# The last 128 gated tokens of each half stay on chip, two units move ahead of half B's last down block, and a norm gets four row tiles

## The chip, the cores and the metric

One core of a Trainium2 chip. The time is that of one execution on the device in microseconds (us), as the median of several runs; one execution is recorded by the hardware profiler. PE is TensorE (matmul), DVE is VectorE, ACT is ScalarE, POOL is GpSimd, SP is SyncE, which here only issues DMAs.

## The reference

A trunk of two layers over 1024 tokens of 1024 numbers, each with a feed-forward network (FFN) behind it, and a last norm. Layer 0 mixes tokens with a gated MLP and with running means, layer 1 is an RWKV-7 time mixing. All is fp32. What the change touches is the end of the time mixing:

```python
y = wkv7_scan(rh, decay, kh, vh, -kk, kk * ah)
mean = jnp.mean(y, axis=-1, keepdims=True)
var = jnp.mean(jnp.square(y - mean), axis=-1, keepdims=True)
y = ((y - mean) * lax.rsqrt(var + GN_EPS)).reshape(bsz, seq, d)
y = y * ln_w.astype(f32) + ln_b.astype(f32)
bonus = jnp.sum(rh * kh * r_k.astype(f32), axis=-1, keepdims=True) * vh
y = (y + bonus.reshape(bsz, seq, d)).astype(h.dtype)
return (y * g) @ w_o, v_first
...
def swiglu(hn, w_gate, w_up, w_down):
    return (jax.nn.silu(hn @ w_gate) * (hn @ w_up)) @ w_down
```

The scan runs over the tokens one after the other, 16 heads of 64. The residual `x + ...` follows, then `rms_norm` and `swiglu` with 2816 hidden columns.

## The kernel before

**Halves.** The 1024 tokens are worked on as half A (0 to 511) and half B (512 to 1023). Arrays lie with the features on the 128 partitions and the tokens along the row, as 8 tiles of 128 x 512 for a half.

**Products.** Every fp32 operand is split into a high and a low part (`split`, L159 to L162: ACT copies the high part, DVE subtracts it for the low one), and a product is three matmuls, high by high, high by low and low by high (`mm3`, L440 to L444, and `quarter`, L777 to L779). A matmul is 128 x 128 by 128 x 512.

**Weights.** Weights of 512 KB come from DRAM into one of three tiles `raw` by DMAs that ACT issues (`load_at`, L125), and are split into `whi` and `wlo`, three tiles each. Their order is a plan that is written out by hand ahead of the work (`push`, `push_units`, `push_o`, `push_act`), and `take` asks for the next one. `o` is the output projection's weight: eight pieces (`m` = 0 to 7), each of four DMAs of 128 KB.

**Order.** Each engine works through its own queue in order. A scheduler sets that order from a modelled time of each instruction, within priorities (`high_priority`) and waits that the code gives; PE's dense work is in the order of the code in some places.

**The recurrence.** `recur(h, ...)` runs the time mixing of a half as 8 chunks of 64 tokens. It is a generator that `drive` steps on beside dense FFN work, so many pieces of the one per piece of the other (`ratio`). After every second chunk `post(jj)` norms the result of 128 tokens (`ysb`), with the reciprocal root by POOL (`rsqrt`, L447), and `turn_out` transposes it on PE (L1540), multiplies by the gate on DVE into `gch` (L1784) and stores 128 tokens in DRAM (`y_d[h]`, L1787). The `yp` products of a chunk are copied to `ysb` by ACT (L1690), which is where this chain starts.

**The output projection.** It needs all 512 tokens of `y`. Four pieces of `y_d[h]` (two of the eight feature tiles each, 512 tokens) come back through `raw`, are planned by `push_act`, and are split by `take_act` into `ahi` and `alo`. `out_proj` then does 8 x 8 products with `o`, and each result is added to the residual `h` (L540).

**Half A.** The recurrence of half A runs beside the layer-0 FFN of half B; the last down block of that FFN (`steps_b`) runs out as the recurrence ends. Then come `project_norm` (the norm of half B for its time mixing, whose row sums are the matmuls of L477 and whose broadcast is L494), the output projection of A, low-rank products and gates of half B (`project_gate`), and `norm_a`: the norm of half A for its FFN by `norm_split` (L510), whose eight rows are scaled by DVE into one of two tiles (tag `nsq`), split, and spilled to `n_d[1]`. The first FFN units of half A use them at once. Mixing rows (L1231, L1238) of half B's projections run on DVE and ACT beside it.

**Half B.** The recurrence of half B runs beside the layer-1 FFN of half A. Near the end, `AHEAD_IN` = 2 units of a second step (`first_steps`, tiles `mm<-ahi,whi` of L777) stand ahead of the last down block of A (48 matmuls), four units behind it, three pieces of y between them. Then come the output projection of half B and the remaining six units beside the norm of half B.

Of the kernel before, what the change touches and what calls it, by code (L numbers as in the profile page):

```python
# [16 lines left out]
P = 128  # L17
# [25 lines left out]
LATER = (5, 6, 7, 8, 9, 10)  # L43
AHEAD_IN = 2


@with_exitstack
def tile_trunk(
# [56 lines left out]
    def col(c):  # L105
        return vec[:, c : c + 1]
# [8 lines left out]
    def push(key, parts, view=lambda t: t, dest=None):  # L115
        plan.append((key, parts, view, dest))

    def load_at(i):
        if i >= len(plan) or i in raws:
            return  # L120
        if plan[i][0][0] in acts and plan[i][0][0] not in dests:
            return
        raw = wst.tile([P, D], F32, tag="raw", name="raw")
        for dst, src in plan[i][1]:
            act.dma_start(dst(raw), src)  # L125
        raws[i] = raw
# [148 lines left out]

    def push_act(key, src):

        acts.add(key)
        for i in range(4):
            yield push((key, i), [(lambda raw: raw.rearrange("p (k t) -> p k t", k=2), src[:, 2 * i : 2 * i + 2, :])],  # L280
                 dest=lambda i=i: dests[key](i))

# [74 lines left out]
    o_first[0]()  # L357
    list(push_act(("y", 0), y_d[0]))
    push_beside(1, [lambda: None] + o_first[1:] + push_f(1, 0, G1A[0]))
# [9 lines left out]
    def push_units(units, between=iter(())):  # L369
        for i, n in units:  # L370
            push(("first1", i, n), push_pair(1, i, n, 0))
            next(between, None)
            next(between, None)

    for e in ffn_events(TAIL, True):
        if e == ("d", TAIL[-1]):
            push_units(UNITS[:AHEAD_IN])
        if e[0] != "d":
            push_ffn_event(1, 0, *e)
    y1 = push_act(("y", 1), y_d[1])  # L380
    push_units(UNITS[AHEAD_IN : AHEAD_IN + 3])
    for unit in (UNITS[AHEAD_IN + 3], None, None):
        next(y1)
        if unit:
            push_units([unit])
    next(y1)
    for go in push_o(1):
        go()
    push_units(UNITS[AHEAD_IN + 4 :])
    for f in range(2 * LATER[0]):  # L390
# [111 lines left out]

    def norm_split(h, c0, pool_, spill=None, b=None):

        if b is None:
            b = norm_scale(h)
        hi, lo = act_tiles(pool_)
        for k in range(KT):
            hn = nt.tile([P, HT], F32, tag="nsq", bufs=2, name="hn")
            dve.scalar_tensor_tensor(  # L510
                out=hn, in0=H[h][:, k, :], scalar=col(c0 + k), in1=b, op0=ALU.mult, op1=ALU.mult
            )
# [1004 lines left out]

    def recur(h, wp, stream, ratio):

# [202 lines left out]
        def post(jj):  # L1722
# [48 lines left out]
            def turn_out():  # L1771
                for q in range(2):
                    o = pst("sm")
                    for i in range(4):
                        p = 4 * q + i // 2 * 2
                        ordered(
                            pe.transpose, o[:, i * P : (i + 1) * P],
                            ysb[i % 2][:, p : p + 2, :].rearrange("t p d -> t (p d)"), ident,
                        )
                    ov = o.rearrange("p (q c r t) -> p q r c t", q=2, c=2, r=2)  # L1780
                    for i in range(4):
                        m = q * 4 + i
                        g = gch[:, m, :].rearrange("p (c t) -> p c t", c=2)
                        dve.scalar_tensor_tensor(  # L1784
                            out=g, in0=ov[:, i // 2, 1 - i % 2], scalar=col(C_LNB + m), in1=g, op0=ALU.add, op1=ALU.mult,
                        )
                sp.dma_start(y_d[h][:, :, jj * P : (jj + 1) * P], gch)  # L1787

# [20 lines left out]
        for c in range(8):  # L1809
            if c % 2 == 1:  # L1810
                pieces[:] = [post(c // 2)]
                next(pieces[0])
            open_[0] = (99, 1)[c % 2]
            bkt, w1 = yield from burst(c, bkt, w1)
            yield BURST
        for _ in pieces[0]:
            yield 0.3
        turned.pop()()
        yield 1.0

# [232 lines left out]
    prime_b()  # L2053
    drive(ffn(0, 1, nxt["hn"], f, D0P[:3], nd=2), recur(0, wp, in_pieces(hb_pool, 1, h_d[1, 0]), 6.2), 6.2)
    wp_es.close()
# [33 lines left out]
    def norm_a(gate):  # L2089
        got = []  # L2090
        between = [lambda: None] * KT
        between[0] = lambda: got.append(row_sums(sums))

        def rows_():
            with tc.high_priority(offset=AHEAD):
                got.append(norm_rows(got[0]))

        between[4] = rows_
        with tc.manual_schedule(engines={mybir.EngineType.PE}):
            gate(between)  # L2100
        with tc.high_priority(offset=AHEAD):
            hnA.extend(norm_split(0, C_FFN + 8, (yhi, y), n_d[1], got[1]))

# [13 lines left out]
    f, f_es = open_pool(name="ffn2", bufs=1, side="right")  # L2117
    hnA = nxt["hn"]
    all_units = [(i, 2 * i, n, True) for i, n in UNITS]
    dense_a = ffn(  # L2120
        1, 0, hnA, f, TAIL, early=True, after=lambda m: sp.dma_start(hs_d[0][:, m, :], H[0][:, m, :]),
        then={TAIL[-1][-1]: lambda: first_steps(all_units[:AHEAD_IN], hnA, f, "first1", hid1_d, True)},
    )
    drive(dense_a, recur(1, wp, in_pieces(hp, 0, h_d[0, 1]), RATIO), RATIO)
    for e in (wp_es, hp_es, f_es, ps_es):
        e.close()
    ps_es = open_psum("psd2", DENSE)
    f, f_es = open_pool(name="ffn3", bufs=1, side="right")
    xa, xa_es = open_pool(name="xa", bufs=1, side="left")
    xb, xb_es = open_pool(name="xb", bufs=1, side="left")  # L2130
    b, b_es = open_pool(name="act3", bufs=1, side="left")
# [4 lines left out]

    def y_calls():
        for call in range(8):
            if call > 4:
                next(got_y)  # L2140
            yield

    exhaust(first_steps(all_units[AHEAD_IN : AHEAD_IN + 4], hnA, f, "first1", hid1_d, between=y_calls()))
    exhaust(got_y)
    acc, add = running_sums(1)

# [175 lines left out]
```

## Time and profile before

| | us |
|---|---|
| median of three runs | 2373.31 |
| lowest and highest | 2365.13, 2375.23 |
| the profiled execution | 2372.49 |
| its span | 2370.8 |
| PE busy in it | 2283.6 |
| DVE busy | 1552.3 |
| ACT busy | 952.7 |
| POOL busy | 181.8 |

The span is the time from the first to the last recorded instruction. Places in the profile are in us from the start of the span. Three of them matter here: 1236 to 1310 (end of half A's recurrence, its output projection, up to the gate), 1323 to 1349 (norm of half A), 1772 to 1803 (end of half B's recurrence and what follows). An entry such as [8.82 <-ACT ahi L161] behind an instruction says that its engine was idle for 8.82 us before it, and that the instruction of ACT at L161 that writes `ahi` let it go on. ACTq and SPq are DMA issues of the two engines.

### The profile page before, as it was taken

The page shows a single profiled execution, that of the slowest core. Times are in us where ns is not written, and L with a number is a line of the kernel's source. Part 1 is how long each engine was busy: PE and PEld are TensorE (multiplying, and loading weights), DVE is VectorE, ACT ScalarE, POOL GpSimd, SP SyncE. Part 2 cuts the span into 40 slices and gives each one's busy share as a digit, 9 for nine tenths or more (in the row PEclk, how much of TensorE's full clock was granted, in tenths as well). Part 3 has the DMA queues.
Part 4 walks back from the last instruction along what each step waited for, and adds up shares of the span by engine and source line. Part 5 has one row for each costly group of instructions (what it writes and reads, how often), then busy time and mean ns, then how long its engine had stood idle before and what let it go on. Part 6 is the DMA issues. An engine that isn't in the chain of part 4 may idle for free. (4 is left out here: it accounts for less than half of the span.)

```text
span 2370.8 us, 37920 instructions
## 1 busy us (share of the span) xinstructions
PE 2283.6 (96%) x15171; PEld 1861.3 (79%) x15171; DVE 1552.3 (65%) x2496; ACT 952.7 (40%) x1507; POOL 181.8 (8%) x207
## 2 busy tenths in 40 slices
PE   8999999999999999999989899999999999999998
PEld 6888888888888877778767678777777887787886
DVE  6445775555567957767767857766664564776565
ACT  6233443443223764433335655533333442332014
POOL 0200000000000022201100122200110000000002
PEclk9999999999999999999999999999999999999999
DMA  5114473333765465776445375676546674547342
GB/s 183 54 45 141 152 196 98 107 107 121 286 234 200 149 187 146 210 219 195 129 141 154 121 211 152 194 232 175 161 147 212 203 249 142 169 151 257 125 160 98
DMA packets 427985, 392.04 MB, mean 165 GB/s; under 512 B 96992, under 2 KB 358240, under 8 KB 425120
## 3 DMA queue, kind: packets, MB, share of 16 engines
q1 hardware_dynamic: 174752, 202.68, 26.9%
q10 hardware_dynamic: 251840, 182.74, 25.9%
q0 software_dynamic: 1216, 4.20, 0.8%
q8 instruction: 119, 1.95, 0.3%
q14 instruction: 58, 0.48, 0.1%
HBM read 283.25 MB, written 106.30 MB: 164 GB/s over the span
## 5 line engine op out<-in xcount | busy, mean ns | idle before, releaser
L161 ACT ACTIVATE whi<-raw 128x1024 fp32r<-128x1024 f32 (+2 forms) x274 | 265.1, 974 | 394.2 <-PE mm L443 212.0
L162 DVE TENSOR_TENSOR wlo<-raw,whi 128x1024 fp32r<-128x1024 f32 (+2 forms) x274 | 314.1, 1151 | 164.8 <-ACT whi L161 135.8
L443 PE MATMUL mm<-alo,whi 128*128 128x512 f32 x864 | 342.2, 396 | 2.4 <-DVE alo L162 2.1
L442 PE MATMUL mm<-ahi,whi 128*128 128x512 f32 x832 | 329.4, 399 | 13.1 <-ACT ahi L161 11.5
L444 PE MATMUL mm<-ahi,wlo 128*128 128x512 f32 x832 | 328.7, 395 | 2.9 <-DVE wlo L162 2.9
L540 DVE TENSOR_TENSOR h<-h,mm 128x512 f32<-128x512 f32 x268 | 180.4, 685 | 133.8 <-PE mm L444 125.0
L777 PE MATMUL mm<-ahi,whi 128*128 128x512 f32 x488 | 193.0, 396 | 5.6 <-ACT whi L161 5.2
L442 PEld LDWEIGHTS mm<-ahi,whi 128*128 128x128 f32 x832 | 157.1, 189 | 50.7 <-ACT ahi L161 12.8
L443 PEld LDWEIGHTS mm<-alo,whi 128*128 128x128 f32 x864 | 163.3, 189 | 41.2 <-DVE alo L162 5.7
L778 PE MATMUL mm<-alo,whi 128*128 128x512 f32 x488 | 191.1, 392 | 0.0
L779 PE MATMUL mm<-ahi,wlo 128*128 128x512 f32 x488 | 188.7, 391 | 0.0
L444 PEld LDWEIGHTS mm<-ahi,wlo 128*128 128x128 f32 x832 | 157.2, 189 | 38.5 <-DVE wlo L162 3.8
L442 PE MATMUL mm<-hd,dhi 128*128 128x512 f32 x368 | 144.4, 392 | 1.1 <-DVE h L540 1.1
L444 PE MATMUL mm<-hd,dlo 128*128 128x512 f32 x368 | 143.4, 390 | 0.0
L443 PE MATMUL mm<-hd,dhi 128*128 128x512 f32 x368 | 143.2, 389 | 0.0
L777 PEld LDWEIGHTS mm<-ahi,whi 128*128 128x128 f32 x488 | 92.4, 189 | 26.8 <-ACT whi L161 6.1
L161 ACT ACTIVATE dhi<-raw 128x1024 fp32r<-128x1024 f32 x40 | 40.5, 1052 | 171.7 <-PE mm L443 135.6
L778 PEld LDWEIGHTS mm<-alo,whi 128*128 128x128 f32 x488 | 92.5, 190 | 19.4 <-issue 0.5
L779 PEld LDWEIGHTS mm<-ahi,wlo 128*128 128x128 f32 x488 | 92.3, 189 | 19.5
L442 PEld LDWEIGHTS mm<-hd,dhi 128*128 128x128 f32 x368 | 69.1, 188 | 16.3 <-DVE h L540 1.9
L444 PEld LDWEIGHTS mm<-hd,dlo 128*128 128x128 f32 x368 | 69.1, 188 | 14.5
L443 PEld LDWEIGHTS mm<-hd,dhi 128*128 128x128 f32 x368 | 69.1, 188 | 14.4 <-issue 0.2
(438 smaller groups left out, 4762.7 us busy)
## 6 DMA issues: line engine op xcount, KB each, us to landing
raw<-in_ffn_w_down_dram ACTq DMA_DIRECT2D x76, 512.0 KB
hid_d<-hid SPq DMA_DIRECT2D x69, 512.0 KB
raw<-in_ffn_w_gate_dram ACTq DMA_DIRECT2D x68, 512.0 KB
raw<-in_ffn_w_up_dram ACTq DMA_DIRECT2D x68, 512.0 KB
hd<-hid_d SPq DMA_DIRECT2D x56, 512.0 KB
ar<-ab_d SPq DMA_DIRECT2D x16, 1024.0 KB
raw<-in_ab_w_in_dram ACTq DMA_DIRECT2D x16, 512.0 KB
raw<-in_ab_w_out_dram ACTq DMA_DIRECT2D x16, 512.0 KB
```

Of the source, the lines that this page charges most:

```text
L161: act.activation(hi, src, AF.Copy)
L162: (eng or dve).tensor_tensor(out=lo, in0=src, in1=hi.bitcast(F32), op=ALU.subtract)
L442: pe.matmul(o, whi, xhi, start=first, stop=False)
L443: pe.matmul(o, whi, xlo, start=False, stop=False)
L444: newest[0] = pe.matmul(o, wlo, xhi, start=False, stop=last).ins
L540: dve.tensor_tensor(out=H[h][:, m, :], in0=H[h][:, m, :], in1=o, op=ALU.add)
L777: pe.matmul(o, wh[:, k, :], x[0][:, k, :], start=st, stop=False, skip_group_check=True)
L778: pe.matmul(o, wh[:, k, :], x[1][:, k, :], start=False, stop=False, skip_group_check=True)
L779: pe.matmul(o, wl[:, k, :], x[0][:, k, :], start=False, stop=k == 3, skip_group_check=True)
```

## The change

The first three parts of `y` that `turn_out` gives (tokens 0 to 383 of a half) go to DRAM as before. The fourth (`jj` = 3) is written to two on-chip tiles `yend` of 128 x 4 x 128, one for each four feature tiles, and `split_end` splits it into the last 128 columns of `ahi` and `alo`, at high priority. The pieces that come back from DRAM have 384 tokens. In half A, `yend` lies in a pool of its own; in half B, in the two tiles of tag `nsq`.

Of the four DMAs of each weight `o`, the second and fourth are issued by SP.

`AHEAD_IN` is 4, so four units stand ahead of half B's last down block and two behind it, with the pieces of y between these. In the recurrence of half B the last pause is put elsewhere: the transposes of `turn_out` are ordered behind the newest dense matmul after 2.7 pieces more of dense work.

`norm_a` uses the two `yend` tiles for rows 0, 1, 4 and 5, beside the two `nsq` tiles for the others. Two pools (`xa` and `xb`) are opened in the other order. Line numbers of the changed code are 5 or 6 lower in this part (L535 for L540, L1751 for L1756), and higher at the end.

```diff
-AHEAD_IN = 2
+AHEAD_IN = 4
...
-            act.dma_start(dst(raw), src)
+        for n, (dst, src) in enumerate(plan[i][1]):
+            (sp if plan[i][0][0] == "o" and n % 2 else act).dma_start(dst(raw), src)
...
-    def push_act(key, src):
+    def push_act(key, src, n=HT):
...
-            yield push((key, i), [(lambda raw: raw.rearrange("p (k t) -> p k t", k=2), src[:, 2 * i : 2 * i + 2, :])],
+            yield push((key, i), [(lambda raw: raw.rearrange("p (k t) -> p k t", k=2)[:, :, :n], src[:, 2 * i : 2 * i + 2, :n])],
...
-    list(push_act(("y", 0), y_d[0]))
+    list(push_act(("y", 0), y_d[0], HT - P))
...
-    y1 = push_act(("y", 1), y_d[1])
-    push_units(UNITS[AHEAD_IN : AHEAD_IN + 3])
-    for unit in (UNITS[AHEAD_IN + 3], None, None):
-        next(y1)
-        if unit:
-            push_units([unit])
-    next(y1)
+    push_units(UNITS[AHEAD_IN : AHEAD_IN + 2], push_act(("y", 1), y_d[1], HT - P))
...
-    push_units(UNITS[AHEAD_IN + 4 :])
+    push_units(UNITS[AHEAD_IN + 2 :])
...
-            hn = nt.tile([P, HT], F32, tag="nsq", bufs=2, name="hn")
+            pl, tag = extra if extra and k % 4 < 2 else (nt, "nsq")
+            hn = pl.tile([P, HT], F32, tag=tag, bufs=2, name="hn")
...
-                        g = gch[:, m, :].rearrange("p (c t) -> p c t", c=2)
+                        g, to = (t.rearrange("p (c t) -> p c t", c=2) for t in (gch[:, m, :], end(m) if jj == 3 else gch[:, m, :]))
...
-                sp.dma_start(y_d[h][:, :, jj * P : (jj + 1) * P], gch)
+                if jj != 3:
+                    sp.dma_start(y_d[h][:, :, jj * P : (jj + 1) * P], gch)
...
-            yield BURST
+            if c < 7 or not h:
+                yield BURST
...
+        if h:
+            yield 2.7 * ratio
+            last.append(newest[0])
         turned.pop()()
...
+    def split_end(ys, ends):
+        with tc.high_priority(offset=AHEAD):
+            for q, t in enumerate(ends):
+                split(t, *(y[:, 4 * q : 4 * q + 4, HT - P :] for y in ys))
...
         yield from take_act(("y", h))
+        split_end(ys, end_a.tiles)
...
-            hnA.extend(norm_split(0, C_FFN + 8, (yhi, y), n_d[1], got[1]))
+            hnA.extend(norm_split(0, C_FFN + 8, (yhi, y), n_d[1], got[1], (yhi, "yend")))
...
-    exhaust(first_steps(all_units[AHEAD_IN : AHEAD_IN + 4], hnA, f, "first1", hid1_d, between=y_calls()))
+    exhaust(first_steps(all_units[AHEAD_IN : AHEAD_IN + 2], hnA, f, "first1", hid1_d, between=got_y))
     exhaust(got_y)
+    split_end(ys, end_b.tiles)
```

How this moves instructions, by the order in which each engine has them (xN counts equal ones in a row). On ACT, at the end of half A's recurrence, where `nsq<-h` (L455, after it L449) belongs to `project_norm`, before:

```order
L455 ACTIVATE nsq<-h 128x512 x5
L125 DMA raw<-y_d_81 128x1024 x3
L455 ACTIVATE nsq<-h 128x512 x2
L161 ACTIVATE ahi<-raw 128x1024 x2
L125 DMA raw<-y_d_81 128x1024
L161 ACTIVATE ahi<-raw 128x1024
L125 DMA raw<-in_rwkv_w_o_dram 64x4x128 x4
L161 ACTIVATE ahi<-raw 128x1024
```

and after:

```order
L125 DMA raw<-y_d_81 128x2x384
L161 ACTIVATE ahi<-raw 128x2x384
L446 ACTIVATE nacc<-h 128x512
L449 ACTIVATE nsq<-h 128x512
L125 DMA raw<-y_d_81 128x2x384
L449 ACTIVATE nsq<-h 128x512 x2
L161 ACTIVATE ahi<-raw 128x2x384
L161 ACTIVATE ahi<-yend 128x4x128 x2
L449 ACTIVATE nsq<-h 128x512
L125 DMA raw<-y_d_81 128x2x384
L125 DMA raw<-in_rwkv_w_o_dram 64x4x128 x2
L161 ACTIVATE ahi<-raw 128x2x384
```

The first piece of y (not in these rows) and the next two are loaded and split ahead of the end of the norm's squares; only the fourth load stands behind the splits of `yend`.

On SP, from there on (`h<-h_d` reloads half A's residual, `h_d<-h` stores half B's), before:

```order
L2050 DMA h_d_86<-h 128x512 x5
L1787 DMA y_d_81<-gch 1024x1x128
L2050 DMA h_d_86<-h 128x512 x3
L2071 DMA h<-h_d_83 128x1024 x4
L515 DMA n_d_88<-hn 128x512 x8
```

and after:

```order
L2067 DMA h_d_86<-h 128x512 x7
L125 DMA raw<-in_rwkv_w_o_dram 64x4x128 x3
L2067 DMA h_d_86<-h 128x512
L125 DMA raw<-in_rwkv_w_o_dram 64x4x128 x9
L2089 DMA h<-h_d_83 128x1024 x4
L125 DMA raw<-in_rwkv_w_o_dram 64x4x128 x2
L510 DMA n_d_88<-hn 128x512 x8
```

The store of the last 128 tokens is gone, and the reload of the residual stands behind 14 transfers of `o` (two of them ahead of these rows).

On DVE, in the norm of half A, before:

```order
L510 SCALAR_TENSOR_TENSOR hn<-h,vec,aux 128x512
L162 TENSOR_TENSOR alo<-hn,ahi 128x512
L1238 SCALAR_TENSOR_TENSOR mix<-hn_11129,vec,mix 128x512 x2
L510 SCALAR_TENSOR_TENSOR hn<-h,vec,aux 128x512
L162 TENSOR_TENSOR alo<-hn,ahi 128x512
L1231 TENSOR_TENSOR xlo<-mix,xhi 128x512 x2
```

and after:

```order
L505 SCALAR_TENSOR_TENSOR hn<-h,vec,aux 128x512 x3
L1226 TENSOR_TENSOR alo<-mix,ahi 128x512
L505 SCALAR_TENSOR_TENSOR hn<-h,vec,aux 128x512
L1226 TENSOR_TENSOR alo<-mix,ahi 128x512
L162 TENSOR_TENSOR alo<-hn,ahi 128x512 x3
L1233 SCALAR_TENSOR_TENSOR mix<-hn_11134,vec,mix 128x512
L162 TENSOR_TENSOR alo<-hn,ahi 128x512
L505 SCALAR_TENSOR_TENSOR hn<-h,vec,aux 128x512
```

Rows come in groups, and part of the mixing stands behind them.

On DVE, at the end of half B's recurrence (`h<-h,mm` are the down block's additions to the residual), before:

```order
L540 TENSOR_TENSOR h<-h,mm 128x512 x3
L1756 SCALAR_TENSOR_TENSOR mean<-mean,var 128x16
L1762 TENSOR_TENSOR ysb<-ysb,var 128x512
L1763 TENSOR_TENSOR ysb<-ysb,mean 128x512
L1766 TENSOR_TENSOR ysb<-ysb,lnw 128x512
L1767 TENSOR_TENSOR ysb<-ysb,vch 128x512
L1766 TENSOR_TENSOR ysb<-ysb,lnw 128x512
L1767 TENSOR_TENSOR ysb<-ysb,vch 128x512
L1784 SCALAR_TENSOR_TENSOR gch<-sm,vec,gch 128x128 x8
```

and after:

```order
L535 TENSOR_TENSOR h<-h,mm 128x512 x3
L1751 SCALAR_TENSOR_TENSOR mean<-mean,var 128x16
L1757 TENSOR_TENSOR ysb<-ysb,var 128x512
L535 TENSOR_TENSOR h<-h,mm 128x512
L1758 TENSOR_TENSOR ysb<-ysb,mean 128x512
L535 TENSOR_TENSOR h<-h,mm 128x512
L1761 TENSOR_TENSOR ysb<-ysb,lnw 128x512 x2
L1762 TENSOR_TENSOR ysb<-ysb,vch 128x512 x2
L1779 SCALAR_TENSOR_TENSOR yend<-sm,vec,gch 128x128 x8
L162 TENSOR_TENSOR alo<-yend,ahi 128x4x128 x2
```

Two additions of the down block now stand within the chain to `ysb`. On PE, 43 matmuls of that block stand between the last `yp` products and the transposes instead of 30, and behind the transposes 48 matmuls of units come before the output projection's 80 in a row.

More of the change, by code (lines that the diff above doesn't have):

```diff
@@ L123, in load_at @@
         raw = wst.tile([P, D], F32, tag="raw", name="raw")
-        for dst, src in plan[i][1]:
-            act.dma_start(dst(raw), src)
+        for n, (dst, src) in enumerate(plan[i][1]):
+            (sp if plan[i][0][0] == "o" and n % 2 else act).dma_start(dst(raw), src)
         raws[i] = raw
@@ L274, in push_proj @@
                     next(pieces, None)
-    def push_act(key, src):
+    def push_act(key, src, n=HT):
         acts.add(key)
         for i in range(4):
-            yield push((key, i), [(lambda raw: raw.rearrange("p (k t) -> p k t", k=2), src[:, 2 * i : 2 * i + 2, :])],
-                 dest=lambda i=i: dests[key](i))
+            yield push((key, i), [(lambda raw: raw.rearrange("p (k t) -> p k t", k=2)[:, :, :n], src[:, 2 * i : 2 * i + 2, :n])],
+                 lambda t: t.rearrange("p (k t) -> p k t", k=2)[:, :, :n], dest=lambda i=i: dests[key](i))
     def groups_of(first):
@@ L501, in act_tiles, with norm_split @@
         return [(pool_[i] if type(pool_) is tuple else pool_).tile([P, KT, n], F32R, tag=t, name=t) for i, t in enumerate(("ahi", "alo"))]
-    def norm_split(h, c0, pool_, spill=None, b=None):
+    def norm_split(h, c0, pool_, spill=None, b=None, extra=None):
         if b is None:
@@ L1516, in tile_trunk, with recur @@
     state_d = dram.tile([P, 8, 64], F32, name="state_d")
-    def recur(h, wp, stream, ratio):
+    def recur(h, wp, stream, ratio, end):
         def wt(tag, bufs, shape):
@@ L1782, in turn_out @@
                         m = q * 4 + i
-                        g = gch[:, m, :].rearrange("p (c t) -> p c t", c=2)
+                        g, to = (t.rearrange("p (c t) -> p c t", c=2) for t in (gch[:, m, :], end(m) if jj == 3 else gch[:, m, :]))
                         dve.scalar_tensor_tensor(
-                            out=g, in0=ov[:, i // 2, 1 - i % 2], scalar=col(C_LNB + m), in1=g, op0=ALU.add, op1=ALU.mult,
+                            out=to, in0=ov[:, i // 2, 1 - i % 2], scalar=col(C_LNB + m), in1=g, op0=ALU.add, op1=ALU.mult,
                         )
-                sp.dma_start(y_d[h][:, :, jj * P : (jj + 1) * P], gch)
+                if jj != 3:
+                    sp.dma_start(y_d[h][:, :, jj * P : (jj + 1) * P], gch)
             turned.append(turn_out)
@@ L1821, in tile_trunk, with ends_of, end @@
     early_o = {}
+    def ends_of(pool_, tag):
+        def end(m):
+            if m % 4 == 0:
+                end.tiles.append(pool_.tile([P, 4, P], F32, tag=tag, bufs=2, name="yend"))
+            return end.tiles[m // 4][:, m % 4, :]
+        end.tiles = []
+        return end
+    def split_end(ys, ends):
+        with tc.high_priority(offset=AHEAD):
+            for q, t in enumerate(ends):
+                split(t, *(y[:, 4 * q : 4 * q + 4, HT - P :] for y in ys))
     def with_first(h):
@@ L2045, in tile_trunk @@
     yhi, yhi_es = open_pool(name="y0hi", bufs=1, side="left")
+    end_a = ends_of(yhi, "yend")
     hb_pool, hb_es = open_pool(name="hb1", bufs=1, side="left")
@@ L2053, in tile_trunk @@
     prime_b()
-    drive(ffn(0, 1, nxt["hn"], f, D0P[:3], nd=2), recur(0, wp, in_pieces(hb_pool, 1, h_d[1, 0]), 6.2), 6.2)
+    drive(ffn(0, 1, nxt["hn"], f, D0P[:3], nd=2), recur(0, wp, in_pieces(hb_pool, 1, h_d[1, 0]), 6.2, end_a), 6.2)
     wp_es.close()
@@ L2060, in tile_trunk @@
     drive(steps_b)
+    exhaust(between[0])
     f_es.close()
@@ L2118, in tile_trunk @@
     hnA = nxt["hn"]
+    end_b = ends_of(nt, "nsq")
     all_units = [(i, 2 * i, n, True) for i, n in UNITS]
@@ L2123, in tile_trunk @@
     )
-    drive(dense_a, recur(1, wp, in_pieces(hp, 0, h_d[0, 1]), RATIO), RATIO)
+    drive(dense_a, recur(1, wp, in_pieces(hp, 0, h_d[0, 1]), RATIO, end_b), RATIO)
     for e in (wp_es, hp_es, f_es, ps_es):
@@ L2128, in tile_trunk @@
     f, f_es = open_pool(name="ffn3", bufs=1, side="right")
+    xb, xb_es = open_pool(name="xb", bufs=1, side="left")
     xa, xa_es = open_pool(name="xa", bufs=1, side="left")
-    xb, xb_es = open_pool(name="xb", bufs=1, side="left")
     b, b_es = open_pool(name="act3", bufs=1, side="left")
@@ L2135, in tile_trunk @@
     got_y = take_act(("y", 1))
[L2137 to L2141, printed above, removed]
-    exhaust(first_steps(all_units[AHEAD_IN : AHEAD_IN + 4], hnA, f, "first1", hid1_d, between=y_calls()))
+    exhaust(first_steps(all_units[AHEAD_IN : AHEAD_IN + 2], hnA, f, "first1", hid1_d, between=got_y))
     exhaust(got_y)
+    split_end(ys, end_b.tiles)
     acc, add = running_sums(1)
@@ L2163, in norm_b @@
             yield 1.0
-    drive(first_steps(all_units[AHEAD_IN + 4 :], hnA, f, "first1", hid1_d), norm_b(norm_bcast(acc[0])), 2.0)
+    drive(first_steps(all_units[AHEAD_IN + 2 :], hnA, f, "first1", hid1_d), norm_b(norm_bcast(acc[0])), 2.0)
     hb_es.close()
@@ L2245, in tile_trunk @@
             load_hid(0, None)
-    for e in (wp_es, f_es, b_es, xb_es, xa_es, ps_es):
+    for e in (wp_es, f_es, b_es, xa_es, xb_es, ps_es):
         e.close()
```

## The prediction

> **What bounds the kernel now.** I read the page's busy times first, then PE's rows in order of time for its idle stretches at the places that the change touches, then the granted clock behind each stretch, then what released PE there.
>
> ```profile
> PE 2283.6 (96%) x15171; PEld 1861.3 (79%) x15171; DVE 1552.3 (65%) x2496; ACT 952.7 (40%) x1507; POOL 181.8 (8%) x207
> ```
>
> PE is the bound: 2370.8 - 2283.6 = 87 us of the span is all that it idles. The change adds and removes no dense matmul, so it can win only idle time of PE, and time in which PE runs slowly. These are PE's rows at the three places (start, duration, then in brackets the idle time ahead of it and its releaser):
>
> ```profile
> 1244.98 0.79 PE L442 MATMUL mm<-ahi,whi 128*128 128x512 f32 x1 [8.82 <-ACT ahi L161]
> 1248.14 0.63 PE L442 MATMUL mm<-ahi,whi 128*128 128x512 f32 x1
> 1248.56 0.63 PE L443 MATMUL mm<-alo,whi 128*128 128x512 f32 x1
> 1251.65 0.39 PE L444 MATMUL mm<-ahi,wlo 128*128 128x512 f32 x1
> 1251.88 0.39 PE L442 MATMUL mm<-ahi,whi 128*128 128x512 f32 x1
> 1257.07 0.50 PE L442 MATMUL mm<-ahi,whi 128*128 128x512 f32 x1 [1.63 <-ACT whi L161]
> 1260.16 0.55 PE L444 MATMUL mm<-ahi,wlo 128*128 128x512 f32 x1 [2.36 <-DVE wlo L162]
> 1310.25 0.39 PE L442 MATMUL mm<-xhi,whi 128*128 128x512 f32 x1
> 1326.67 0.96 PE L442 MATMUL mm<-ahi,whi 128*128 128x512 f32 x3 [2.67 <-ACT ahi L161]
> 1332.62 0.50 PE L443 MATMUL mm<-alo,whi 128*128 128x512 f32 x1 [0.99 <-DVE alo L162]
> 1348.63 0.39 PE L444 MATMUL mm<-ahi,wlo 128*128 128x512 f32 x1
> 1776.44 0.45 PE L1540 MATMUL sm<-ident,ysb 128*128 128x128 f32 x1 [3.74 <-DVE ysb L1767]
> 1777.97 1.30 PE L1540 MATMUL sm<-ident,ysb 128*128 128x128 f32 x5 [1.08 <-DVE ysb L1767]
> 1798.97 0.50 PE L777 MATMUL mm<-ahi,whi 128*128 128x512 f32 x1 [4.19 <-ACT whi L161]
> ```
>
> The first stretch, 1236.17 to 1310.25, is half A's output projection and what follows it up to the gate. It idles 8.82 + 1.63 + 2.36 = 12.8 us. The second is the norm of half A, where each row of eight waits for DVE. The third is the end of half B's recurrence: 3.74 + 1.08 + 4.19 = 9.0, for which I take 9.4 with the small waits behind it.
>
> Each long wait has a second price. The view by stretches shows it (stretch, length, busy time of PE, PEld, DVE, ACT and POOL, then the granted clock, DMA share and GB/s):
>
> ```profile
> 1236.17:1310.25 74.08, 61.27 (x251) 49.46 (x251) 57.08 (x80) 43.38 (x65) 1.20 (x2) 0.91 0.57 166
> 1244.98:1250.26 5.28, 5.28 (x16) 4.52 (x17) 4.33 (x5) 2.21 (x3) 1.01 (x1) 0.50 0.52 174
> 1260.16:1263.50 3.34, 3.34 (x9) 2.61 (x10) 3.34 (x5) 3.34 (x7) 0.00 (x0) 0.55 1.01 380
> 1326.67:1333.00 6.33, 4.97 (x14) 2.99 (x15) 6.27 (x10) 4.75 (x8) 0.14 (x1) 0.73 0.39 137
> 1776.44:1783.00 6.56, 5.48 (x17) 4.50 (x18) 3.51 (x10) 0.00 (x0) 0.00 (x0) 0.52 0.75 295
> 1798.97:1803.40 4.43, 4.19 (x11) 3.03 (x12) 2.33 (x4) 2.34 (x4) 0.00 (x0) 0.61 0.57 195
> ```
>
> Behind waits of 8.82, 2.36, 2.67, 3.74 and 4.19 us the clock is half to three quarters. Matmuls start 0.42 us apart (1248.14 to 1248.56) instead of 0.23 (1251.65 to 1251.88): 0.2 us more for each of about 8, so 1.6 us for a wait.
>
> [...]
>
> **Part 1, half A: y's last 128 tokens on chip, o's weights on two queues.** Before, the chain runs over DRAM:
>
> ```profile
> 1232.85 2.16 DVE L1784 SCALAR_TENSOR_TENSOR gch<-sm,vec,gch 128x128 f32<-128x128 f32 x8
> 1235.04 0.54 SPq L1787 DMA_DIRECT2D y_d<-gch  x1
> 1238.64 1.48 ACTq L125 DMA_DIRECT2D raw<-y_d  x3
> 1243.88 2.26 ACT L161 ACTIVATE ahi<-raw 128x1024 fp32r<-128x1024 f32 x2 [2.56 <-DMA raw<-y_d]
> 1247.43 2.60 ACTq L125 DMA_DIRECT2D raw<-in_rwkv_w_o_dram  x4
> 1250.17 1.06 ACT L161 ACTIVATE ahi<-raw 128x1024 fp32r<-128x1024 f32 x1 [2.51 <-DMA raw<-y_d]
> ```
>
> Gating ends at 1235.0, the store is issued, all four loads of y wait for it, and the first split starts at 1243.88. Afterwards the loads need tokens 0 to 383 alone, whose stores were issued a chunk pair earlier. The order puts three of the four loads and splits ahead of the end of the last down block, and splits `yend` straight behind the gating. PE can begin at about 1236.4. Only the fourth piece is late: it waits for a `raw` buffer, which the split of the first sets free. Issued at about 1238 and split some 5 us later (1238.64 to 1243.88 for the first piece now), it is there at 1243. PE has 3 of 4 pieces, 18 matmuls of 0.23 = 4.1 us, so it waits 1.8 there. With 0.2 ahead and the splits behind (0.6, 0.5, 0.7) I count 4 us; the bounds are 0 (all four early) and 8.82 (the row now). The weights: four issues of o take ACT 2.60 us, of which half now go to SP. I count nothing for that on the end, since ACT's splits, not its issues, come last here; the second weight's low part still costs 1.3 (bounds 0 and the 2.36 of now). The reload of H, behind 14 of o's transfers on SP, and the low-rank weight behind it: 2.0 (bounds 0 and 4.28, below).
>
> The stretch (first row of the view above) is busy for 61.27 of 74.08 us. Its 240 matmuls of 0.227 us and the small ones are 57.3 at full clock, so 4.0 is slow clock. Before 12.8 + 4.0 = 16.8, after 4.0 + 1.3 + 2.0 = 7.3 of short waits: **gain 9.5** (from 4 to 13). The added splits of `yend` (2 on ACT, 2 on DVE) replace as much width in the pieces, so they cost nothing in sum.
>
> **Part 2, four row tiles.** DVE's rows of the norm now:
>
> ```profile
> 1331.23 0.74 DVE L510 SCALAR_TENSOR_TENSOR hn<-h,vec,aux 128x512 f32<-128x512 f32 x1
> 1332.49 1.41 DVE L1238 SCALAR_TENSOR_TENSOR mix<-hn,vec,mix 128x512 f32<-128x512 f32 x2
> 1333.81 0.74 DVE L510 SCALAR_TENSOR_TENSOR hn<-h,vec,aux 128x512 f32<-128x512 f32 x1
> 1344.57 1.49 DVE L162 TENSOR_TENSOR alo<-hn,ahi 128x512 fp32r<-128x512 f32 x2
> ```
>
> A row takes 2.58 us (1331.23 to 1333.81), in which two instructions of the mixing (1.32) stand between: DVE fills the wait for one of two tiles with them. PE has 9 matmuls of 0.227 = 2.05 us a row, so it starves. With four tiles the order has 10 mixing instructions between the first row and the last `alo` instead of 17: 7 x 0.65 = 4.6 us earlier, which PE's end at 1348.6 + 0.4 follows, less 0.2 for the first row's unchanged wait: **gain 4.4** (0, if DVE waits for the spill's stores out of the new tiles; 5, if PE is let run). The mixing that is put off comes in the next units, where DVE has room as long as they need three projections of PE per piece.
>
> **Part 3, half B.** The end of the last chunk now, with two rows of the queues:
>
> ```profile
> 1770.03 2.90 POOL L447 TENSOR_TENSOR var<-var,small 128x16 f32<-128x16 f32 x1 [19.17 <-DVE var L1752]
> 1777.13 0.69 DVE L1767 TENSOR_TENSOR ysb<-ysb,vch 128x512 f32<-128x512 f32 x1
> 1778.88 2.16 DVE L1784 SCALAR_TENSOR_TENSOR gch<-sm,vec,gch 128x128 f32<-128x128 f32 x8 [1.06 <-PE sm L1540]
> 1781.07 0.54 SPq L1787 DMA_DIRECT2D y_d<-gch  x1
> 1785.98 0.34 ACTq L125 DMA_DIRECT2D raw<-y_d  x1
> 1796.92 0.33 ACTq L125 DMA_DIRECT2D raw<-y_d  x1
> ```
>
> PE has 30 matmuls of the down block (6.8 us) ahead of the transposes, and the chain through POOL's power, ACT and DVE to `ysb` takes longer: it waits 3.74 + 1.08 = 4.8. Afterwards 43 stand there (9.75 us). The chain is 4.8 + 6.8 = 11.6, and two residual additions of 0.69 now stand within it: about 12.6. The wait is 12.6 - 9.75 = 2.85, with 0.4 behind it 3.3. It is long enough for a slow clock by the row of 2.36: 1.6 again. The second wait, 4.19, came from y's last load (issued at 1796.92, once a buffer was free) and the splits and o's weight queued behind it on ACT. Afterwards 48 matmuls of two units (10.9 us) cover `yend`'s splits and the fourth piece; I leave 0.8. Before 9.4 + 2.6 of slow clock (1.6 and 1.0) = 12.0, after 3.3 + 1.6 + 0.8 = 5.7: **gain 6.3** (3, if the chain is as late as now; 10, if both waits go). The two units moved ahead of the down block are neither added nor removed, and they run at full clock in both places: nothing. Two y loads now stand on ACT's queue ahead of the last chunk's steps, behind the landing of y's third store. That is 4.9 us from issue to load in half B's last (1781.07 to 1785.98); bounds 0 and 4.9, and I take 0, since by the order it is issued ahead of the last chunk's burst.
>
> Sum: 9.5 + 4.4 + 6.3 = 20.2 us. The profiled execution took 2372.49 (span 2370.8), 0.8 below the median of the three runs, 2373.31: 2372.5 - 20.2 = 2352.3, and against the median 2353.
>
> **Rivals.** Some 0.5% (12 us: 2361.4 and 2385) is what a measurement of this kernel can tell from no change.
>
> ```profile
> 1253.62 1.41 DVE L1155 SCALAR_TENSOR_TENSOR hn<-h,vec,aux 128x512 f32<-128x512 f32 x2 [1.13 <-PE aux L494]
> 1299.73 1.22 DVE L162 TENSOR_TENSOR wlo<-raw,whi 128x1024 fp32r<-128x1024 f32 x1 [7.99 <-ACT whi L161]
> 1255.09 4.28 SPq L2071 DMA_DIRECT2D h<-h_d  x4
> ```
>
> DVE becomes the bound of half A. The norm's broadcast on PE (L494) moves from behind 18 matmuls of the projection to behind 76, so it comes at about 1236.4 + 76 x 0.227 + 4 = 1257.7: DVE starts on `hn` some 4 us later than at 1253.62. From there to 1346 it is idle but for the 7.99 us ahead of 1299.73. If those 8 us absorb the 4, my sum holds with 4 us to spare, of which the earlier gate asks some; if they stay, the norm starts 4 us later than now, which part 2's 4.4 makes up, and only part 3 is left: 2373.3 - 6.3 = 2367 (no change). For it: 8 us is little. Against it: that idle time ended on a weight's split, which comes earlier when PE does.
>
> The fourth y piece lands no earlier than the last one now (1250.17): PE waits about 7 more in part 1, and the time is near 2359.
>
> The clock stays whole behind half B's 2.85 us: 1.6 us less, 2351.4. [...]
>
> Slower: SP's queue holds its head. The H reload, 4.28 us of issues at 1255.09, stands behind 14 of o's transfers, of which the last wait for `raw` buffers that come free with the weight five back. The residual additions of the output projection need H and hold PSUM, and PE with it. Each us that the reload is issued later than about 1265 costs one us; from 1285 it eats the whole sum, and from 1297 the kernel is slower by over 0.5%; when all weights of o had to pass first, about 1300, it would be 2388. Against it: the weights are split one per 5.4 us of matmuls from 1240 on, so the sixth buffer is free at about 1265.
>
> **Chances.** Forecast 0.64, whole clock 0.04, late fourth piece 0.12, DVE-bound 0.16, SP 0.04. Of the forecast's 0.64 some 0.04 ends above 2361.4. Faster 0.60 + 0.04 + 0.12 = 0.76; same 0.04 + 0.16 = 0.20; slower 0.04. The ends: the parts' best gains together (13 + 5 + 10 = 28) give 2345, and 2 for the spread of the runs 2343. At the top the late piece and half of the DVE case are within 2366, which leaves 0.12 above and about 0.06 below.
>
> **What would show it.** Part 1: PE's first `mm<-ahi,whi` of the output projection near 1236.4 rather than 1244.98, short waits with full clock, and the gate at about 1300.8 rather than 1310.25. Part 2: the last `alo<-hn` 4 to 5 us earlier measured from the first row. Part 3: one wait of about 3 us ahead of the transposes and none of 4 behind. Wrong I would be if DVE's idle stretch ahead of the gate stayed at 8 us, if SP's `h<-h_d` came behind 1265, or if ACT waited for `raw<-y_d` ahead of the last chunk's XT.

## The result, and the profile after

The changed kernel takes 2345.93 us (median of four runs, 2344.05 to 2347.14), the kernel before 2372.16 in the runs of the same comparison. The ratio is 0.9895, 95% interval 0.9879 to 0.9911: 1.05% or 25 us less (21 to 29). The forecast was 2353 within 2343 to 2366. The profiled execution of the changed kernel has a span of 2343.1 us.

Busy time of the engines in the changed kernel:

```profile
PE 2277.5 (97%) x15171; PEld 1859.1 (79%) x15171; DVE 1548.8 (66%) x2500; ACT 953.1 (41%) x1511; POOL 181.5 (8%) x207
```

PE has the same 15171 matmuls and is busy for 6.1 us less (2283.6 before). The span is 27.7 shorter, so PE's idle time fell from 87.2 to 65.6 us, by 21.6. Both prices of a wait fell, the idle time and the slow clock behind it: the mean granted clock is 0.991, 0.988 before. Of the 27.7 us, 5.2 lie ahead of the first of the three places, and they are not shown to come from the change (see "Before, once more").

PE's rows at the three places, which answer to those shown of before (line numbers are lower by 5 or 6):

```profile
1230.80 0.39 PE L436 MATMUL mm<-ahi,whi 128*128 128x512 f32 x1
1233.11 0.71 PE L437 MATMUL mm<-alo,whi 128*128 128x512 f32 x1 [1.92 <-DVE alo L162]
1240.93 0.50 PE L436 MATMUL mm<-ahi,whi 128*128 128x512 f32 x1 [0.70 <-ACT whi L161]
1242.19 0.50 PE L438 MATMUL mm<-ahi,wlo 128*128 128x512 f32 x1 [0.53 <-DVE wlo L162]
...
1316.67 0.97 PE L436 MATMUL mm<-ahi,whi 128*128 128x512 f32 x3 [1.16 <-ACT ahi L161]
1319.80 0.80 PE L437 MATMUL mm<-alo,whi 128*128 128x512 f32 x1 [2.16 <-DVE alo L162]
...
1768.88 0.30 PE L1535 MATMUL sm<-ident,ysb 128*128 128x128 f32 x1 [3.23 <-DVE ysb L1762]
1769.48 1.73 PE L1535 MATMUL sm<-ident,ysb 128*128 128x128 f32 x7 [0.30 <-DVE ysb L1762]
1778.10 0.50 PE L772 MATMUL mm<-ahi,whi 128*128 128x512 f32 x1 [0.76 <-ACT t L817]
```

In half A the output projection begins where the down block ends, without the 8.82 us; waits of 1.92, 0.70, 0.53 and (at 1273.94) 0.82 are left of 12.8. In the norm a wait of 0.46 and two larger ones are left, 1.16 ahead of a block of three matmuls on three rows and 2.16 behind it. In half B a wait of 3.23 ahead of the transposes is left, and the largest behind them is 0.76 instead of 4.19.

How much each stage gave can't be read as a difference of two places, since the executions differ before the first moved instruction already (below). So I take the lengths of three stretches, each from an event of the program to another: A, from the end of the down block that runs out with half A's recurrence to the gate's first matmul; N, from the last low-rank matmul ahead of the norm to the first `mm<-hidhi,whi` behind it; B, from the first product `sm<-XT,gt` of half B's recurrence to the first `mm<-ahi,s3hi` far behind it, between which PE has the same 3919 instructions in every kernel. "N to B" is the time between the last two stretches, "start" is where stretch A begins. All in us, of one profiled execution of each kernel:

| kernel | start | A | N | N to B | B |
|---|---|---|---|---|---|
| before | 1236.0 | 74.2 | 31.6 | 247.0 | 406.5 |
| before, again | 1230.3 | 75.6 | 31.6 | 246.4 | 405.9 |
| changed | 1230.8 | 63.7 | 29.9 | 249.7 | 395.0 |
| changed, again | 1234.1 | 63.4 | 28.9 | 249.0 | 395.9 |
| half A's part alone | 1235.5 | 66.3 | 29.8 | 249.0 | 407.3 |
| half B's part alone | 1232.1 | 75.7 | 31.6 | 244.3 | 397.6 |
| norm's tiles alone | 1236.9 | 75.9 | 28.9 | 249.7 | 406.3 |
| changed, two norm tiles | 1230.9 | 63.5 | 30.8 | 249.4 | 400.8 |
| changed, o on ACT alone | 1232.1 | 66.2 | 29.8 | 246.8 | 398.1 |
| changed, half B's y by DRAM | 1232.4 | 63.7 | 30.0 | 250.4 | 406.2 |
| changed, other norm rows | 1230.5 | 63.7 | 28.4 | 245.5 | 393.6 |
| the same, again | 1232.7 | 63.5 | 28.4 | 247.6 | 394.7 |

Against the two profiles of before (means 74.9, 31.6, 406.2) the changed kernel's first profile has 11.2 less in A, 1.7 in N, 11.2 in B: 24.1. But it has about 3 more between N and B, so some 21 us are left of it, at the lower end of the interval. One place stands out there: PE waits for `k`, which DVE writes late.

```profile
1386.60 1.68 PE L1331 MATMUL bo<-ind,k 128*128 128x2 f32 x8 [2.20 <-DVE k L1430]
```

Half clock follows it for 6.83 us (granted clock 0.50 from 1386.83 to 1393.66). Seven of the twelve profiles have this wait (1.36 to 2.75 us), and they take 247.6 to 250.4 from N to B; the five without it, among them both of before, take 244.3 to 247.0. DVE itself waits there for POOL's `sg` (4.72 us, 2.35 before). Every kernel that has the wait has half A's part or the norm's tiles, but two profiles of such kernels are without it, so what brings it is not shown.

### The profile page after: what moved, and what is told of

The parts are those of the page before. It is cut to its first block, busy times and chain, and to the rows that moved or that the text cites. A ratio compares the mean times of both kernels' runs of the same rounds, so it can differ in the third digit from the quotient of the medians.

```text
span 2343.1 us, 37955 instructions
## 1 busy us (share of the span) xinstructions
PE 2277.5 (97%) x15171; PEld 1859.1 (79%) x15171; DVE 1548.8 (66%) x2500; ACT 953.1 (41%) x1511; POOL 181.5 (8%) x207
## 4 chain that ended last, share of the span: by engine, by line
PE 78%; DVE 9%; DMA 6%; ACT 2%; issue 2%; POOL 2%; SPq 0%; ACTq 0%; POOLq 0%; DVEq 0%
PE mm L436 13%; PE mm L437 13%; PE mm L438 13%; PE mm L772 10%; PE mm L773 10%; PE mm L774 9%; PE sm L1535 4%; DVE wlo L162 1%; DVE it L1487 1%; DVE xi L1492 1%; ACT whi L161 1%; PE yp L1535 1%; DVE h L535 1%; PE mm L623 1%; PE mm L622 1%
## 5 line engine op out<-in xcount | busy, mean ns | idle before, releaser
L535 DVE TENSOR_TENSOR h<-h,mm 128x512 f32<-128x512 f32 x268 | 179.7, 684 | 125.9 <-PE mm L438 118.7
L774 PEld LDWEIGHTS mm<-ahi,wlo 128*128 128x128 f32 x488 | 91.8, 188 | 19.1
```

Of the source, the lines that this page charges most:

```text
L535: dve.tensor_tensor(out=H[h][:, m, :], in0=H[h][:, m, :], in1=o, op=ALU.add)
L774: pe.matmul(o, wl[:, k, :], x[0][:, k, :], start=False, stop=k == 3, skip_group_check=True)
```

## The experiments

**Half A's part alone.** The kernel before with `end_a` and 384-token pieces in half A only.

```diff
-    list(push_act(("y", 0), y_d[0]))
+    list(push_act(("y", 0), y_d[0], HT - P))
...
+        split_end(ys, end_a.tiles)
```

> The kernel before with half A's part alone: the last 128 tokens of half A on chip and split from there, y's pieces of 384 tokens; half B, the norm's row tiles and o's queue as before. Theory 1 (the wait at the hand-off was the landing of y's last store, and the freed time stays freed): 10 us less than before, 2362, PE waits at most 2.5 us at the start of the output projection. Theory 2 (DVE's full stretch behind it takes the time back): less than 3 us of gain, 2369 or more, with DVE's idle stretch ahead of the gate still near 8 us.

Measured: 2360.87 us, ratio 0.9956 (0.9938 to 0.9974), 10 us less than before (6 to 15). Stretch A is 66.3 us long instead of 74.9. PE's first wait there:

```profile
1237.76 0.50 PE L443 MATMUL mm<-alo,whi 128*128 128x512 f32 x1 [1.69 <-DVE alo L162]
```

The wait is 1.69 instead of 8.82, and the time stays freed: theory 1. DVE's idle stretch of 7.99 us ahead of the gate is gone too. In its rows from 1252 to 1325 no wait is over 2.34 us, so it absorbed the shift and did not become the bound. N is 29.8 in this kernel, with two row tiles as before: half A's part alone takes 1.8 us out of the norm's stretch.

**Half B's part alone.** The kernel before with `AHEAD_IN`, the transposes' new place and `end_b`.

```diff
-AHEAD_IN = 2
+AHEAD_IN = 4
...
+            yield 2.7 * ratio
+            last.append(newest[0])
...
+    split_end(ys, end_b.tiles)
```

> The kernel before with half B's part alone: four units ahead of the last down block, the transposes ordered later, half B's last 128 tokens on chip; half A, the norm's row tiles and o's queue as before. Theory 1 (the prediction's sum: waits 9.4 + slow clock 2.6 become 5.7): 6 us less, 2366. Theory 2 (the changed place of the units also takes small waits out of the recurrence ahead of it, as the profile after suggests): 9 to 11 us less, 2362.

Measured: 2361.5 us, ratio 0.9968 (0.9947 to 0.9988), 8 us less (3 to 13). Both theories' times lie in the interval. Stretch B is 8.6 shorter than before. Theory 2's mechanism falls: the recurrence of this kernel has the small waits as before,

```profile
1693.28 0.66 PE L1535 MATMUL sm<-ident,ar 128*128 128x128 f32 x4 [0.75 <-DVE gt L1576]
1695.17 0.34 PE L1535 MATMUL sm<-ident,ysb 128*128 128x128 f32 x1 [1.23 <-DVE ysb L1762]
```

while the kernel with half A's part alone has no wait over 0.3 between 1628 and 1760. These waits come and go with something other than the units; what, no run here tells. The hand-off of the kernel with half B's part is not the forecast one either: PE doesn't wait ahead of the transposes at all, and waits 2.45 us (at 1793.71) for the first weight of the output projection.

The ratios of the two parts multiply to 0.9956 x 0.9968 = 0.9924.

**The norm's tiles alone, and the change without them.** The same edit, once put into the kernel before, once taken out of the changed kernel.

```diff
-            hn = nt.tile([P, HT], F32, tag="nsq", bufs=2, name="hn")
+            pl, tag = extra if extra and k % 4 < 2 else (nt, "nsq")
+            hn = pl.tile([P, HT], F32, tag=tag, bufs=2, name="hn")
```

> The kernel before with four row tiles for half A's norm alone. Theory 1 (the prediction's term): 4.4 us less, 2368. Theory 2 (rows come in blocks, PE waits once for a whole block, and the slow clock behind that wait eats most): 0 to 2 us less, 2371; a wait of about 2 us in the norm, with half-speed matmuls behind it.

> The changed kernel with two row tiles for half A's norm again, all else as changed. Theory 1 (the prediction's term): 4.4 us more than the changed kernel's 2345.9, 2350. Theory 2 (the tiles are worth 1 to 2 us): 2347 to 2348.

Measured: the tiles alone 2372.07 us, ratio 1.0006 (0.9991 to 1.002); the change without them 2351.03, ratio 0.9924 (0.9901 to 0.9946), just the product of the two halves' parts. By totals the tiles are worth between nothing (the first) and 0.3% or 7 us (0.9924 against 0.9895, whose intervals meet), so the totals don't settle it. The table tells more. N falls from 31.6 to 28.9 in the first pair, from 30.8 to 29.9 in the second, 0.9 to 2.7 us, and the forecast's 4.4 isn't reached in either. In the first pair the time from N to B grows by 2.7 to 3.3 (with a wait for `k` of 2.16), which leaves nothing, as the total has it. In the second pair the excess of the kernel without the tiles stands mostly in B, 400.8 against 395.0, far from the norm. So its 2351.03, close to theory 1's 2350, is no sign for theory 1. The waits are as theory 2 had them (2.21 us in the kernel with the tiles alone), and this is the clock behind the 2.16 us one in the changed kernel (stretch, length, busy PE, PEld, DVE, ACT, POOL, granted clock, DMA share, GB/s):

```profile
1319.80:1325.46 5.66, 5.66 (x13) 4.51 (x14) 5.66 (x10) 2.78 (x6) 0.00 (x0) 0.51 0.18 67
```

13 matmuls take 5.66 us at a granted clock of 0.51; at full clock, 0.23 us from one to the next (1325.46 to 1325.69), they would take 3.0.

**All of o's transfers on ACT.**

```diff
-            (sp if plan[i][0][0] == "o" and n % 2 else act).dma_start(dst(raw), src)
+            act.dma_start(dst(raw), src)
```

> The changed kernel with all of o's transfers issued by ACT again. Theory 1 (the prediction: splits, not issues, come last on ACT, so the second queue is worth nothing): 2345 to 2347, and the stretch from the end of the down block to the gate stays at 63.7 us. Theory 2 (ACT's 2.6 us of issues for each weight delay its splits): 2 to 3 us more, 2348 to 2349, the stretch at 66.3 us, as in the run with half A's part alone, which issued them all from ACT.

Measured: 2346.62 us, ratio 0.99 (0.9886 to 0.9915), against 0.9895: no difference in the totals, as theory 1 has it. But stretch A is 66.2 us, as theory 2 has it. The profile shows where: the second weight's split comes later,

```profile
1242.45 0.50 PE L436 MATMUL mm<-ahi,whi 128*128 128x512 f32 x1 [1.23 <-ACT whi L161]
```

1.23 where 0.70 stands in the changed kernel, and PE waits further for `h` (0.84 at 1269.62) on its way to the gate. So the second queue gives 2.5 us in its stretch (the two kernels with all of `o` on ACT and half A's tiles on chip have 66.2 and 66.3, the six with the second queue 63.4 to 63.7). That it doesn't show in the medians is no contradiction, since the intervals leave 3 us either way.

**Half B's last tokens by DRAM, with all else as changed.** PE's order is that of the changed kernel.

```diff
-    push_units(UNITS[AHEAD_IN : AHEAD_IN + 2], push_act(("y", 1), y_d[1], HT - P))
+    push_units(UNITS[AHEAD_IN : AHEAD_IN + 2], push_act(("y", 1), y_d[1]))
...
-    split_end(ys, end_b.tiles)
```

> The changed kernel with half B's last 128 tokens through DRAM again and pieces of 512 tokens; the four units ahead of the down block, the transposes' place and PE's order stay as changed. Theory 1 (the tiles on chip are what takes the 4.19 us wait away; 48 matmuls, 10.9 us, don't cover a store, its landing and four pieces): 8 to 14 us more, 2354 to 2360, with one long wait of PE behind the units. Theory 2 (the cover does it, wherever y lies): 0 to 2 us more, 2346 to 2348.

Measured: 2355.72 us, ratio 0.9944 (0.9929 to 0.9958), 10 us more than the changed kernel. Stretch B is 406.2, no shorter than before: theory 1. First PE's row, then those of SP and ACT:

```profile
1779.91 0.80 PE L772 MATMUL mm<-ahi,whi 128*128 128x512 f32 x1 [4.23 <-ACT t L817]
```

```profile
1773.11 0.54 SPq L1783 DMA_DIRECT2D y_d<-gch  x1
1777.62 0.83 ACTq L125 DMA_DIRECT2D raw<-y_d  x2
1779.26 0.60 ACT L817 ACTIVATE t<-mm 128x512 f32<-128x512 f32 x1 [11.22 <-issue]
1781.45 1.06 ACT L161 ACTIVATE ahi<-raw 128x1024 fp32r<-128x1024 f32 x1 [1.60 <-DMA raw<-y_d]
1793.91 1.06 ACT L161 ACTIVATE whi<-raw 128x1024 fp32r<-128x1024 f32 x1 [0.18 <-DMA raw<-in_rwkv_w_o_dram]
```

The loads of y wait on ACT's queue for the store to land (4.0 us from the end of its issue to the first load), and `t<-mm`, which copies a unit's result out of its PSUM tile, stands behind them; PE waits for it. The first weight of `o` is split at 1793.91, 24 us behind the first transpose; in the changed kernel at 1781.64, 13 us behind it. So the units moved ahead are no cover by themselves: the tiles on chip take the store and its landing out of ACT's queue, and with that the wait.

**Other rows in the extra tiles.**

```diff
-            pl, tag = extra if extra and k % 4 < 2 else (nt, "nsq")
+            pl, tag = extra if extra and k % 2 == 0 else (nt, "nsq")
```

> The changed kernel with the extra tiles used for every second row (0, 2, 4, 6) instead of rows 0, 1, 4 and 5, so that no three rows stand in one block ahead of their low parts. Theory 1 (the waits of 1.16 and 2.16 us and the slow clock come from the block of three): 1 to 3 us less, 2343 to 2345. Theory 2 (DVE's work between the rows is the limit): within 1 us of 2346.

Measured: 2341.9 us, ratio 0.9886 (0.9869 to 0.9902). N is 28.4 us, 1.5 less than in the changed kernel, and the first waits of PE in it are

```profile
1310.44 0.73 PE L436 MATMUL mm<-ahi,whi 128*128 128x512 f32 x2 [0.44 <-ACT ahi L161]
1311.68 0.50 PE L438 MATMUL mm<-ahi,wlo 128*128 128x512 f32 x1 [0.50 <-DVE wlo L162]
1312.94 0.56 PE L437 MATMUL mm<-alo,whi 128*128 128x512 f32 x1 [0.53 <-DVE alo L162]
1319.48 0.50 PE L437 MATMUL mm<-alo,whi 128*128 128x512 f32 x1 [0.54 <-DVE alo L162]
```

The waits of 1.16 and 2.16 are gone in this profile, which looks like theory 1. Both kernels were run again beside each other for the total:

> The changed kernel with the extra tiles for rows 0, 2, 4 and 6, a second time and in more rounds beside the changed kernel. Theory 1 (the norm's stretch, 1.5 us shorter in the profile, is all): 1.5 us less than the changed kernel of the same call. Theory 2 (the 4 us between the medians 2341.9 and 2345.9 are the row order's): 3 to 5 us less.

> The changed kernel once more, unchanged, as the other side of that comparison: 2346 by its four runs so far; spread of the stretch ahead of the change, the down block's end of half A, between 1230 and 1233 us.

Measured: 2343.91 us, ratio 0.989 (0.9874 to 0.9906), for the other rows, 2345.68, ratio 0.99 (0.9886 to 0.9913), for the changed kernel: 1.8 us apart, with intervals of 4 us either way. The stretch is again 28.4, against 28.9 now. But the second profile of the other rows has the long wait again, at the same place:

```profile
1321.52 0.50 PE L437 MATMUL mm<-alo,whi 128*128 128x512 f32 x1 [2.13 <-DVE alo L162]
```

DVE's fourth low part starts 13.1 us behind the first row in the first profiles of both orders, and PE waits for it. So theory 1 of the first run isn't shown: the wait of 2 us doesn't need the block of three. What differs in both profiles of the other rows are three waits of 0.4 to 0.5 where the changed kernel has 0.46 and 1.16, and the clock (granted clock 0.94 in N in the first profile, 0.89 in the first of the changed kernel; matmuls 0.43 us apart behind the long wait in the changed kernel's second, 0.23 apart behind it in this second one). The 3 to 5 us that theory 2 of the second run asks for are not seen again in the totals; a gain of 0.5 to 1.5 in the stretch is. The start lay at 1234.1 in the changed kernel, a little outside of the expected 1230 to 1233.

**Before, once more.**

> The kernel before once more, for a second profile. In the profile after, the stretch before the first moved instruction took some 5 us less than in the profile before. Theory 1 (that is the spread between executions): this profile may lie anywhere between, the down block's end of half A at 1231 to 1237 us and the wait of 2.66 us ahead of the products bo near 861 us gone or smaller. Theory 2 (it goes with the kernel): the end at 1236 to 1237 us and the wait there again.

Measured: 2366.42 us, span 2364.7, and the start at 1230.3 instead of 1236.0: theory 1. The products `bo`, which waited before (first row, of the first profile), don't wait now (second row):

```profile
863.68 0.49 PE L1336 MATMUL bo<-ind,k 128*128 128x2 f32 x3 [2.66 <-DVE k L1435]
```

```profile
859.92 1.03 PE L1336 MATMUL bo<-ind,k 128*128 128x2 f32 x8
```

So the 5.2 us by which the changed kernel was ahead at the start of stretch A lie within the spread of executions of one kernel, and in its own second profile the changed kernel is ahead by only 1.9. They would have been counted for half A, had one taken the difference of two places.

## Why the prediction was right, and where its terms were off

The direction, the three places and the mechanisms of the two halves came as forecast, the norm's did not, and the time lies in the range: 2345.9 against 2353, 25 us of gain against 20.2. By the steps:

**Half A, forecast 9.5.** Stretch A is 10.5 shorter than in the profile that the sum was made against, 11.2 against the mean of two. The waits left were put at 7.3, and these rows show the idle and the slow clock apart:

```profile
1230.79:1294.48 63.69, 59.63 (x252) 47.05 (x250) 52.99 (x76) 37.67 (x58) 1.20 (x2) 0.97 0.57 159
```

PE idles 63.69 - 59.63 = 4.1 us. The 57.3 of busy time that the sum took for full clock is too low: the two profiles with other norm rows have full clock all through this stretch (the first a granted clock of 1.00 from 1230 to 1300, the second matmuls 0.23 us apart), and PE is busy for 58.6 to 58.7 us. So the slow clock is 1.0 here, and was 61.3 - 58.6 = 2.7 before and not 4.0. Those two are no shorter (63.7 and 63.5): they idle for 5.0 and 4.9, since PE, at full clock, waits longer for the next operands. Half clock behind the first wait cost nothing in this stretch.

That the sum came so near is luck in part. The tiles on chip gave less than 9.5, 7.9 against the sum's profile in half A's part alone, and the second queue for `o`'s weights, counted as nothing, gave 2.5. The wait left at the start (1.8 forecast, 1.92 measured) agrees by chance: the forecast put it behind 18 matmuls, for the fourth piece of y, and its own terms give 1243 - 1236.4 - 4.1 = 2.5. It stands behind the first matmul, and what ends it is a low part `alo` of DVE. No wait ends on the fourth piece.

**The norm, forecast 4.4.** Measured 1.7 between the two profiles, 0.9 to 2.7 over the pairs. This step failed, in two ways. It counted 17 instructions between DVE's first row and last `alo` before, which are 15 of the mixing and 2 others, against 10 of the mixing after, where the 2 others stand as well. So 5 go and not 7: 5 x 0.65 = 3.3 us, and 3.5 is what DVE is earlier by. Its first row before, then its rows in the changed kernel:

```profile
1323.85 0.74 DVE L510 SCALAR_TENSOR_TENSOR hn<-h,vec,aux 128x512 f32<-128x512 f32 x1
1306.00 1.40 DVE L505 SCALAR_TENSOR_TENSOR hn<-h,vec,aux 128x512 f32<-128x512 f32 x2
1315.22 2.05 DVE L505 SCALAR_TENSOR_TENSOR hn<-h,vec,aux 128x512 f32<-128x512 f32 x3
1319.06 1.89 DVE L162 TENSOR_TENSOR alo<-hn,ahi 128x512 fp32r<-128x512 f32 x3
1324.05 0.68 DVE L162 TENSOR_TENSOR alo<-hn,ahi 128x512 fp32r<-128x512 f32 x1
```

From the first row to the end of the last `alo` it takes 18.7 us instead of 22.2. And the step took DVE's last `alo` for PE's end. But the three low parts of the middle rows come one right behind the other, from 1319.06, so PE stands still ahead of them and then runs 13 matmuls at half clock. It has 66 matmuls left there to the end of the stretch, which take longer than DVE's remaining rows: PE ends 13.2 us behind DVE's last `alo`, 9.4 before. So the end follows from the stop in the middle and not from DVE's last row. Even the 1.7 is not the tiles' alone, since half A's part by itself takes 1.8 out of N, and some 3 us come back between N and B. The forecast had DVE with room there, and PE does wait for DVE's `k`; that the mixing that is put off is what delays `k` isn't shown.

**Half B, forecast 6.3.** Stretch B is 11.2 to 11.6 shorter. The waits came as forecast: 3.23 + 0.30 against 3.3, and 0.76 against 0.8. (Its sum for the chain has a slip: 11.6 and two additions of 0.69 are 13.0 and not 12.6, so that the first wait is 3.2 by its own terms, as measured.) What was too small is the price of the clock. The rows of the hand-off before, and after, with their clock:

```profile
1765.68:1807.00 41.32, 32.08 (x124) 25.17 (x124) 19.16 (x42) 12.94 (x22) 2.90 (x1) 0.88 0.68 219
```

```profile
1755.58:1784.00 28.42, 24.13 (x101) 19.21 (x101) 20.09 (x46) 11.39 (x21) 2.90 (x1) 0.94 0.79 249
```

0.12 of 41.3 us is 5.0, 0.06 of 28.4 is 1.7: 3.3 of difference, where the forecast had 2.6 - 1.6 = 1.0. Another 2 to 3 us come from small waits of the recurrence ahead of it (4.6 in the profile before, 2.4 after), which the kernel with half B's part alone keeps and the one with half A's part alone has not. But in the latter B is no shorter (407.3), since PE comes to the transposes earlier and waits there 7.80 us instead of 3.74:

```profile
1767.96 0.45 PE L1541 MATMUL sm<-ident,ysb 128*128 128x128 f32 x1 [7.80 <-DVE ysb L1768]
```

So these waits are a gain only where the hand-off behind them is covered too. What makes them come and go stays open.

**The rivals.** DVE as the bound of half A: the broadcast did come later, at 1254.62, 23.8 us behind the end of the down block instead of 16.6. But the idle 7.99 us vanished, as the forecast asked for. The queue of SP:

```profile
1257.34 4.27 SPq L2089 DMA_DIRECT2D h<-h_d  x4
```

The reload comes at 1257.3, 26.5 us behind the down block's end instead of 19.1. The 1265 from which it was to cost is 1259.8 here, as this execution is 5.2 us ahead, so it is still early enough. The late fourth piece did not come: the first wait is 1.92, with 0.70 and 0.53 behind it.

**The clock.** The forecast took 1.6 us for each wait of 2 us or more, by the row of 2.36 us. Behind waits of equal length the runs show both. In the changed kernel a wait of 1.92 us (up to 1233.11) is followed by half clock; in the one with two norm tiles, one of 1.93 at the same place of the program (up to 1233.23) by full clock. The stretches behind the two waits, of the changed kernel, then of the one with two norm tiles:

```profile
1233.23:1236.64 3.41, 3.41 (x9) 2.67 (x10) 3.41 (x6) 0.02 (x1) 0.00 (x0) 0.50 0.58 157
1233.23:1236.24 3.01, 3.01 (x12) 2.17 (x12) 3.01 (x5) 0.00 (x0) 0.00 (x0) 1.00 0.56 150
```

The norm shows both as well: a granted clock of 0.51 behind the wait of 2.16 in the changed kernel, and matmuls 0.23 us apart behind that of 2.13 in the second profile of the other rows. So the length alone doesn't decide; what does is not shown. 3.41 us at 0.50 hold the work of 1.7, which is near the forecast's 1.6 for a wait.

## What to carry to other kernels

With half B's y by DRAM, a store that is read back at once cost more than its landing (10 us in all, against 4.0 from the end of its issue to the first load): the loads that waited for it held ACT's queue, and all that stood behind. Count a wait of the bounding engine with the clock that the profile shows behind it (5.66 us for 13 matmuls in the norm, 3.0 at full clock), unless later waits take back what a full clock would give (half A's stretch, 63.7 us with both), and cut a chain where the engine's order has other work ready, but ask for the largest stop in the middle and not only for the last producer's end. And compare lengths of stretches between events of the program, in two profiles of each kernel, before a difference of a few us is given to a cause, and look at the stretch behind as well: what a stage gains can come back as a wait in the next (some 3 us between N and B here).

## What the runs showed of the hardware that I had not expected

A wait of 1.92 us of PE is followed by half clock in one kernel, one of 1.93 by full clock in another (granted clock 0.50 over the next 3.41 us, 1.00 over the next 3.01). In half A's stretch half clock behind the first wait cost nothing (63.4 and 63.7 us with it, 63.5 and 63.7 at full clock). In half B's hand-off the lost clock before was about 5.0 us (0.12 of 41.3) for waits of 9.4. Two executions of the same kernel differed by 5.7 us ahead of the first place that this change touches; one has a wait of 2.66 us there that the other has not.
